# Gated linear attention: the order of full-array and quarter-array products on TensorE

## The chip, the cores and the metric

The kernel runs on one core of a Trainium2 chip. The metric is device time in microseconds (us) of one execution; the median of three runs of the kernel before is 978.45 us. TensorE (PE) multiplies, VectorE (DVE), ScalarE (ACT) and GpSimd (POOL) do the element-wise work, SyncE (SP) issues the DMAs. Each engine has one instruction queue and works it off in order.

## The reference

One layer of a decoder block: a projection, gated linear attention (GLA), block-sparse attention, a merge, cross-attention and a mixture of 32 experts. The change touches GLA alone: 512 rows, 4 heads, keys of 64, values of 128, chunks of 64 rows. Cut to that:

```python
b = jnp.cumsum(log_a, axis=3)
att = jnp.einsum('bhncd,bhnsd->bhncs', q * jnp.exp(b - b_mid), k * jnp.exp(b_mid - b))
att = jnp.where(causal, att, 0.0)
o_intra = jnp.einsum('bhncs,bhnsv->bhncv', att, v)
kv = jnp.einsum('bhncd,bhncv->bhndv', k * jnp.exp(b_last - b), v)
...
_, states = lax.scan(step, init, (jnp.moveaxis(decay, 2, 0), jnp.moveaxis(kv, 2, 0)))
...
o_inter = jnp.einsum('bhncd,bhndv->bhncv', q * jnp.exp(b), states)
o = o_intra + o_inter
```

So a chunk's output is its masked scores times its values, plus its queries times the state that the chunks before it have left. Chunk 0 has no state before it.

## The kernel before

The 512 rows are four tiles (t) of 128, two chunks (c) each. Two heads stand together as a head pair (hp): head 2 hp + half has its 64 key features in partitions 64 half to 64 half + 63. PE's array is 128 by 128: the partitions of the operands are its rows, the partitions of the result its columns. A product whose operands fill 128 partitions and whose result does too takes the full array; the score products take half of the rows (64 partitions in, 128 out); a product with 64 in and 64 out takes a quarter.

`gla()` is a generator. It writes its part of the program in pieces; `weave` puts projection work (`project()`, through `in_feat` and `in_rows`, tiles `fo` and `ro`) between them, as much as the number of each `yield` asks for. The order of the instructions in the queues is the order in which the program is written.

- Scores (lines 547 to 552): for each half, four products k2 by q1, one for each tile, into a PSUM bank `a_ps` of their own; then `copy_predicated` on DVE puts the masked scores into `att[hp]`.
- States (lines 563 to 575): quarter-array products `kv`, 64 rows (a chunk's half of a tile) by 64 columns (half) for chunks 0 to 6, then a scan on DVE into `st[hp]`.
- Outputs (lines 589 to 616): for each tile t two PSUM banks `o_ps0` and `o_ps1`, one for each half, with both head pairs side by side. For each half and hp there is one full-array product (att by vg, all 128 rows of the tile) and behind it one quarter-array product for each of the tile's two chunks (q3 by st; rows by half, columns by the chunk's place in the tile), which adds to what the full one left. Tile 0 has no product for chunk 0. When a half is done, ACT squares it (line 603); then come the row sums on DVE, the power on POOL (line 608), four scalings into `ot` on DVE (line 611), and, one tile later, `finish`: four transposes `ogt` on PE, split by `og.put` on ACT and DVE.

Weights come through `wload` (DMA into `wraw`, issued by SP), are split into `whi` on ACT and `wlo` on DVE by `wsplit`, and are used two blocks later. `load_bias`, behind `gla`, writes a bias table `tbd` to memory and reads it back as `tbias`. Expert weights (`we`) are issued by `eload` as buffers come free.

Of the kernel before, what the change touches and what calls it, by code (L numbers as in the profile page):

```python
# [21 lines left out]
P = 128  # L22
T = 512
NT = T // P
# [41 lines left out]
def bcast_rows(ap, n):  # L66
    return bass.AP(tensor=ap.tensor, offset=ap.offset, ap=[[0, P], [1, n]])
# [3 lines left out]
def block_kernel(ctx, tc, x, mem, g_mem, rel_bias, g_mix, w_in, w_alpha_up, b_alpha, g_gla_head, w_proj_gla,  # L71
# [4 lines left out]
    V, S, G, PE, SY = nc.vector, nc.scalar, nc.gpsimd, nc.tensor, nc.sync  # L76
# [14 lines left out]
    def blk(name, shape, dt=F32):  # L91
        return bp.tile([P] + list(shape), dt, tag="b", name=name)

    def med(name, shape, dt=F32, parts=P):
        return mp.tile([parts] + list(shape), dt, tag="m", name=name)
# [5 lines left out]
    def ps(name, shape, parts=P):  # L101
        return pp.tile([parts] + list(shape), F32, tag="p", name=name)
# [15 lines left out]
    def rows2(name, n, w=T, dt=F32):  # L118

        per = 1024 // w  # L120
        b = [blk(f"{name}{i}", [per, w], dt) for i in range(-(-n // per))]
        return [b[k // per][:, k % per, :] for k in range(n)]
# [12 lines left out]
    def mm(o, l, r, first=True, last=True, **kw):  # L135
        PE.matmul(o, l, r, start=first, stop=last, **kw)  # L136

    def tcol(t):
        return slice(t * P, (t + 1) * P)
# [129 lines left out]
    gmask = first([4, P], U8)  # L269
# [100 lines left out]
    rg, vg, qk = rows2("rg", NT), rows2("vg", NT), rows2("qk", 4)  # L370
# [120 lines left out]
    def gla():  # L491
        at_ps = ps("at_ps", [T], parts=16)
        for t in range(NT):
            PE.transpose(at_ps[:, tcol(t)], alr[:, t, :], ident)
        alrT = med("alrT", [T], parts=17)
        G.memset(alrT, 1.0)
        V.tensor_copy(alrT[0:16, :], at_ps)
        ghb = med("ghb", [512])
        SY.dma_start(ghb, bcast_rows(g_gla_head, 512))
        yield 2.0  # L500
        loga = blk("loga", [NT, 256])
        zz, ab = [], []
        for i in range(2):
            z_ps = ps("z_ps", [2, 256])
            for j in range(2):
                mm(z_ps[:, j, :], alrT[:, tcol(2 * i + j)], wup)
            zz.append(z_ps.rearrange("p a b -> p (a b)"))
            ab.append(med("tmp", [512]))
            S.activation(ab[i], zz[i], AF.Abs)
        for i in range(2):  # L510
            S.activation(ab[i], ab[i], AF.Exp, scale=-1.0)
        for i in range(2):
            S.activation(ab[i], ab[i], AF.Ln, bias=1.0)
            V.scalar_tensor_tensor(loga[:, 2 * i:2 * i + 2, :].rearrange("p a b -> p (a b)"), zz[i], 0.0, ab[i],
                                   op0=ALU.min, op1=ALU.subtract)
        att = [blk(f"att{i}", [2, NT, P]) for i in range(2)]
        for i in range(2):
            G.memset(att[i], 0.0)
        yield "qk"
        q3, k4s, decs, st = [None] * 2, [None] * 2, [None] * 2, [None] * 2  # L520

        def c3(ap):
            return ap.rearrange("p (c t) -> p c t", t=64)

        for hp in range(2):
            b_ps = ps("b_ps", [T])
            for t in range(NT):
                mm(b_ps[:, tcol(t)], loga[:, t, tcol(hp)], tri)
            b_sb, dm, q1, k2 = rows2(f"gw{hp}", 4)
            q3[hp] = med("q3", [512])  # L530
            k4s[hp] = k4 = med("k4", [512])
            S.activation(b_sb, b_ps, AF.Copy, scale=1.0 / 16.0)
            bv = c3(b_sb)
            V.tensor_tensor(c3(dm), bv, bv[:, :, 31:32].to_broadcast([P, 8, 64]), op=ALU.subtract)
            S.activation(q1, dm, AF.Exp)
            S.activation(k2, dm, AF.Exp, scale=-1.0)
            V.tensor_tensor(q1, qk[hp], q1, op=ALU.mult)
            V.tensor_tensor(k2, qk[2 + hp], k2, op=ALU.mult)
            V.tensor_tensor(c3(dm), bv[:, :, 63:64].to_broadcast([P, 8, 64]), bv, op=ALU.subtract)
            S.activation(k4, dm, AF.Exp)  # L540
            V.tensor_tensor(k4, qk[2 + hp], k4, op=ALU.mult)
            decs[hp] = dec = small("dec", [8])
            S.activation(dec, bv[:, :, 63], AF.Exp)
            S.activation(q3[hp], b_sb, AF.Exp)
            V.tensor_tensor(q3[hp], qk[hp], q3[hp], op=ALU.mult)
            yield 6.0
            for half in range(2):
                sl = slice(64 * half, 64 * half + 64)
                a_ps = ps("a_ps", [NT, P])
                for t in range(NT):  # L550
                    mm(a_ps[:, t, :], k2[sl, tcol(t)], q1[sl, tcol(t)])
                V.copy_predicated(att[hp][:, half], gmask, a_ps)
            yield 1.0
            kr_ps = ps("kr_ps", [NT, P])
            for t in range(NT):
                PE.transpose(kr_ps[:, t, :], k4[:, tcol(t)], ident)
            kr = med("kr", [NT, P])
            V.tensor_copy(kr, kr_ps)
            yield GF[hp]
            yield "v"  # L560
            st[hp] = blk(f"st{hp}", [8, P])
            kv_ps = [ps(f"kv{i}", [4, P]) for i in range(2)]
            for c in range(7):
                rs = slice(64 * (c % 2), 64 * (c % 2) + 64)
                for half in range(2):
                    h = 2 * hp + half
                    mm(kv_ps[c % 2][64 * half:64 * half + 64, c // 2, :], kr[rs, c // 2, 64 * half:64 * half + 64],
                       vg[c // 2][rs, tcol(h)], skip_group_check=True)
            for c in range(7):
                kv = kv_ps[c % 2][:, c // 2, :]  # L570
                if c == 0:
                    V.tensor_copy(st[hp][:, 1, :], kv)
                else:
                    V.scalar_tensor_tensor(st[hp][:, c + 1, :], st[hp][:, c, :], dec[:, c:c + 1], kv, op0=ALU.mult,
                                           op1=ALU.add)
            yield 2.0
        for t in range(NT):
            G.tensor_tensor(rg[t], rg[t], ghb, op=ALU.mult)

        def finish(t, ot):  # L580
            t_ps = ps("ogt", [4, P])
            for h in range(4):
                PE.transpose(t_ps[:, h, :], ot[:, h, :], ident)
            og.put(0, tcol(t), t_ps)

        og = Feat("og", 4)
        gla_out.append(og)
        prev = None
        for t in range(NT):
            o_ps = [ps(f"o_ps{half}", [2, P]) for half in range(2)]  # L590
            sq = med("tmp", [4, P])
            for half in range(2):
                sl = slice(64 * half, 64 * half + 64)
                for hp in range(2):
                    h = 2 * hp + half
                    o = o_ps[half][:, hp, :]
                    mm(o, att[hp][:, half, t, :], vg[t][:, tcol(h)], True, False, skip_group_check=True)
                    for c in (2 * t, 2 * t + 1):
                        if c:
                            rs = slice(64 * (c % 2), 64 * (c % 2) + 64)  # L600
                            mm(o[rs], q3[hp][sl, c * 64:(c + 1) * 64], st[hp][sl, c, :], False, c == 2 * t + 1,
                               skip_group_check=True)
                S.activation(sq[:, half:4:2, :], o_ps[half], AF.Square)
            ss = small("ss4", [4])
            V.tensor_reduce(ss, sq, axis=AX.X, op=ALU.add)
            V.tensor_scalar(ss, ss, 1.0 / 128, EPS, op0=ALU.mult, op1=ALU.add)
            rr = small("rr4", [4])
            G.tensor_tensor(rr, ss, neghalf, op=ALU.pow)
            ot = med("ot", [4, P])
            for h in range(4):  # L610
                V.scalar_tensor_tensor(ot[:, h, :], o_ps[h % 2][:, h // 2, :], rr[:, h:h + 1], rg[t][:, tcol(h)],
                                       op0=ALU.mult, op1=ALU.mult)
            yield 2.5
            if prev:
                finish(*prev)
            prev = (t, ot)
        yield 2.0
        finish(*prev)

    fill = project()  # L620
    weave(gla(), fill)
    load_bias()
    drain(fill)
# [103 lines left out]
    for ii in range(4):  # L727
# [4 lines left out]
        for a in range(2):  # L732
            i = 2 * ii + a
# [3 lines left out]
            o = ps("fo", [T])  # L737
            drain(feat(o, gh[:, :, tcol(a)], gl_[:, :, tcol(a)], og.hi, og.lo))
            V.tensor_tensor(zg[i], o, zg[i], op=ALU.mult)
            o = ps("fo", [T])  # L740
# [712 lines left out]
```

## Time and profile before

| | us |
|---|---|
| median of 3 runs (978.40 to 978.49) | 978.45 |
| the profiled execution | 977.96 |
| its span, first to last instruction | 976.1 |
| PE busy | 956.1 (98%) |
| DVE busy | 471.6 (48%) |
| ACT busy | 312.4 (32%) |
| granted TensorE clock, mean | 0.996 |

The span is 1.86 us shorter than the time of the same execution. In a row of the timeline the first number is the start in us from the span's beginning, the second the time from there to the end of the group's last instruction; matmuls are pipelined, so the next row on PE can start before that end, and the difference of two starts is what a group costs. xN counts instructions: a float32 product is two passes on PE, and each is an instruction. In a row of the windows view stand the stretch, its length, then each engine's busy time with the number of instructions, then the granted clock, the busy share of the DMA engines and GB/s. The granted clock is 1.00, the upper of TensorE's two levels, in all stretches used here.

### The profile page before, as it was taken

Reading aid. Unit: us, or ns where it says so; the run is one execution under the profiler, and the core shown is the slowest. Engines: PE = TensorE matmul, PEld = TensorE weight load, DVE = VectorE, ACT = ScalarE, POOL = GpSimd, SP = SyncE. Lnnn points to the kernel's source line nnn. Section 1 sums busy time; section 2 is a strip of 40 time slices with the busy share of each in tenths; the row PEclk is TensorE's granted clock in tenths of the full one; section 3 lists DMA queues with packets and bytes.
Section 4 is the critical chain, followed back from the end, with each engine's and each line's share of the span. In section 5 each row is a group of like instructions: output and inputs, shape, how many; then the busy total and the mean of one; then the engine's idle time right before and its main releaser. Section 6 shows DMA issues by size and latency. Waiting matters only on the chain.

```text
span 976.1 us, 13247 instructions
## 1 busy us (share of the span) xinstructions
PE 956.1 (98%) x4969; PEld 622.3 (64%) x4969; DVE 471.6 (48%) x1047; ACT 312.4 (32%) x639; POOL 32.6 (3%) x46
## 2 busy tenths in 40 slices
PE   8999999999999999999989999999999999999995
PEld 7888778878888888888834445454454543545432
DVE  5344863455556845566743255342544414345224
ACT  6452633445555434465421101111021111201103
POOL 3200010000000000000000000000000000000003
PEclk9999999999999999999999999999999999999998
DMA  9512347223153504473689999999999999999983
GB/s 299 165 44 65 65 58 188 58 80 93 59 181 126 194 25 126 141 264 146 248 313 409 409 409 409 409 409 409 409 409 409 409 409 408 409 409 409 409 319 135
DMA packets 114086, 252.47 MB, mean 259 GB/s; under 512 B 10310, under 2 KB 55651, under 8 KB 114020
## 3 DMA queue, kind: packets, MB, share of 16 engines
q1 hardware_dynamic: 113444, 250.55, 69.8%
q10 hardware_dynamic: 576, 1.05, 0.3%
q8 instruction: 40, 0.66, 0.3%
q14 instruction: 26, 0.21, 0.1%
HBM read 247.90 MB, written 3.67 MB: 258 GB/s over the span
## 4 chain that ended last, share of the span: by engine, by line
PE 92%; DVE 3%; ACT 3%; issue 1%; DMA 1%; SPq 0%; ACTq 0%; POOL 0%; DVEq 0%
PE gu_ps L136 22%; PE y_ps L136 12%; PE fo L131 7%; PE fo L132 7%; PE fo L133 7%; PE g_ps L136 7%; PE c_ps L136 6%; PE ro L133 2%; PE ro L131 2%; PE ro L132 2%; PE x2o L136 2%; PE xo L132 1%; PE xo L133 1%; PE xo L131 1%; PE o_ps L136 1%; PE mo_ps L136 1%
## 5 line engine op out<-in xcount | busy, mean ns | idle before, releaser
L136 PE MATMUL gu_ps<-we,xT 128*64 128x512 f32 x1024 | 229.2, 595 | 1.3 <-DMA we<-in_w_exp_up_dram 0.7
L136 PEld LDWEIGHTS gu_ps<-we,xT 128*64 128x64 f32 x1024 | 70.9, 137 | 135.3 <-issue 121.8
L206 DVE TENSOR_TENSOR wlo<-wraw,whi 128x1024 fp32r<-128x1024 f32 (+1 forms) x71 | 86.0, 1231 | 74.5 <-ACT whi L205 74.3
L136 PE MATMUL y_ps<-we,hid_t 128*64 128x512 f32 x512 | 114.2, 596 | 0.7 <-ACT hid_t L1235 0.7
L1227 DVE SCALAR_TENSOR_TENSOR hid<-hid,ws,gu_ps 128x512 f32<-128x512 f32 x16 | 12.0, 747 | 172.3 <-PE gu_ps L136 172.3
L131 PE MATMUL fo<-hTh,whi 128*128 128x512 f32 x224 | 89.1, 398 | 0.0
L133 PE MATMUL fo<-hTh,wlo 128*128 128x512 f32 x224 | 87.5, 390 | 0.0
L132 PE MATMUL fo<-hTl,whi 128*128 128x512 f32 x224 | 87.5, 390 | 0.0
L1260 DVE TENSOR_TENSOR x<-c_ps,x 128x512 f32<-128x512 f32 x120 | 75.0, 682 | 20.7 <-PE c_ps L136 20.7
L136 PEld LDWEIGHTS y_ps<-we,hid_t 128*64 128x64 f32 x512 | 35.8, 137 | 69.8 <-issue 61.1
L205 ACT ACTIVATE whi<-wraw 128x1024 fp32r<-128x1024 f32 (+2 forms) x73 | 74.4, 1044 | 1.0 <-DMA wraw<-in_w_in_dram 0.7
L136 PE MATMUL g_ps<-oh,xrh 128*128 128x256 f32 x256 | 66.0, 299 | 1.4 <-DVE oh L1025 1.4
L136 PEld LDWEIGHTS g_ps<-oh,xrh 128*128 128x128 f32 x256 | 47.0, 189 | 30.7 <-issue 24.3
L136 PE MATMUL g_ps<-oh,xrl 128*128 128x256 f32 x256 | 61.6, 281 | 0.0
L1226 ACT ACTIVATE hid<-gu_ps 128x512 f32<-128x512 f32 x16 | 9.6, 597 | 157.9 <-PE gu_ps L136 157.9
L205 ACT ACTIVATE yh<-y_ps 128x512 fp32r<-128x512 f32 x32 | 19.1, 598 | 115.1 <-PE y_ps L136 115.1
L1200 ACT ACTIVATE xT<-g_ps,gfeat 128x256 f32<-128x256 f32 x56 | 25.8, 474 | 89.2 <-PE g_ps L136 57.6
L136 PE MATMUL c_ps<-yh,ot 128*128 128x512 f32 x128 | 51.9, 406 | 0.7 <-ACT yh L205 0.7
L136 PE MATMUL c_ps<-yl,ot 128*128 128x512 f32 x128 | 50.6, 395 | 0.2 <-DVE yl L206 0.2
L131 PEld LDWEIGHTS fo<-hTh,whi 128*128 128x128 f32 x224 | 42.1, 188 | 10.1 <-issue 1.9
L133 PEld LDWEIGHTS fo<-hTh,wlo 128*128 128x128 f32 x224 | 42.0, 188 | 9.1
L136 PEld LDWEIGHTS g_ps<-oh,xrl 128*128 128x128 f32 x256 | 47.1, 189 | 0.6
(321 smaller groups left out, 1499.6 us busy)
## 6 DMA issues: line engine op xcount, KB each, us to landing
we<-in_w_exp_gate_dram SPq DMA_DIRECT2D x128, 512.0 KB, 10.2
we<-in_w_exp_up_dram SPq DMA_DIRECT2D x128, 512.0 KB, 10.2
we<-in_w_exp_down_dram SPq DMA_DIRECT2D x128, 512.0 KB, 10.2
wraw<-in_w_in_dram SPq DMA_DIRECT2D x38, 512.0 KB, 3.8
wraw<-in_w_out_dram SPq DMA_DIRECT2D x8, 512.0 KB, 5.0
wraw<-in_w_ckv_dram SPq DMA_DIRECT2D x8, 512.0 KB, 5.1
wraw<-in_w_proj_gla_dram SPq DMA_DIRECT2D x4, 512.0 KB, 4.2
wraw<-in_w_proj_moba_dram SPq DMA_DIRECT2D x4, 512.0 KB, 4.2
```

The source lines that it names most:

```text
L131: PE.matmul(o, lh, rh, start=first, stop=False)
L132: PE.matmul(o, lh, rl, start=False, stop=False)
L133: PE.matmul(o, ll, rh, start=False, stop=last)
L136: PE.matmul(o, l, r, start=first, stop=last, **kw)
L205: S.activation(hi, src, AF.Copy)
L206: eng.tensor_tensor(lo, src, f(hi), op=ALU.subtract)
L1200: S.activation(xT[k], o, AF.Copy, scale=gfeat[:, k:k + 1])
L1226: S.activation(row, gu[0][0:n], AF.Silu)
L1227: V.scalar_tensor_tensor(row, row, ws[:, 0:1], gu[1][0:n], op0=ALU.mult, op1=ALU.mult)
L1260: V.tensor_tensor(xs, o, xs, op=ALU.add)
```

## The change

In the scores both halves' banks are taken first, and the halves alternate from product to product; the mask copies follow when all eight products are written. In the outputs a tile's four full-array products come first, and all its quarter-array products after them. These are ordered by hp, then i, then half, with the chunk chosen so that the two of a step differ in rows (half) and in columns (chunk's place). The squares follow at the end of the tile, one half after the other. The accumulation flags change with it: the first full product of a bank starts it, and the others add. No instruction is added or taken away, and DVE, ACT, POOL and SP keep theirs in the same order.

```diff
@@ -544,12 +544,13 @@
-            for half in range(2):
-                sl = slice(64 * half, 64 * half + 64)
-                a_ps = ps("a_ps", [NT, P])
-                for t in range(NT):
-                    mm(a_ps[:, t, :], k2[sl, tcol(t)], q1[sl, tcol(t)])
-                V.copy_predicated(att[hp][:, half], gmask, a_ps)
+            a_ps = [ps("a_ps", [NT, P]) for half in range(2)]
+            for t in range(NT):
+                for half in range(2):
+                    sl = slice(64 * half, 64 * half + 64)
+                    mm(a_ps[half][:, t, :], k2[sl, tcol(t)], q1[sl, tcol(t)])
+            for half in range(2):
+                V.copy_predicated(att[hp][:, half], gmask, a_ps[half])
@@ -589,17 +590,19 @@
             sq = med("tmp", [4, P])
+            for hp in range(2):
+                for half in range(2):
+                    mm(o_ps[half][:, hp, :], att[hp][:, half, t, :], vg[t][:, tcol(2 * hp + half)], hp == 0, False,
+                       skip_group_check=True)
+            for hp in range(2):
+                for i in range(2):
+                    for half in range(2):
+                        c = 2 * t + (i + half) % 2
+                        sl, rs = (slice(64 * a, 64 * a + 64) for a in (half, c % 2))
+                        if c:
+                            mm(o_ps[half][rs, hp, :], q3[hp][sl, c * 64:(c + 1) * 64], st[hp][sl, c, :], False, True,
+                               skip_group_check=True)
             for half in range(2):
-                sl = slice(64 * half, 64 * half + 64)
-                for hp in range(2):
-                    h = 2 * hp + half
-                    o = o_ps[half][:, hp, :]
-                    mm(o, att[hp][:, half, t, :], vg[t][:, tcol(h)], True, False, skip_group_check=True)
-                    for c in (2 * t, 2 * t + 1):
-                        if c:
-                            rs = slice(64 * (c % 2), 64 * (c % 2) + 64)
-                            mm(o[rs], q3[hp][sl, c * 64:(c + 1) * 64], st[hp][sl, c, :], False, c == 2 * t + 1,
-                               skip_group_check=True)
                 S.activation(sq[:, half:4:2, :], o_ps[half], AF.Square)
```

PE's queue at the score products of head pair 0, before (-) and now (+); the number behind a_ps names the bank, one for each half (a row is a product):

```order
 L133 MATMUL ro1_691<-whi_660,hTl1_150 128x512
-L136 MATMUL a_ps_761<-gw01_709 128x128 x4
-L136 MATMUL a_ps_767<-gw01_709 128x128 x4
+L136 MATMUL a_ps_761<-gw01_709 128x128
+L136 MATMUL a_ps_762<-gw01_709 128x128
+L136 MATMUL a_ps_761<-gw01_709 128x128
+L136 MATMUL a_ps_762<-gw01_709 128x128
+L136 MATMUL a_ps_761<-gw01_709 128x128
+L136 MATMUL a_ps_762<-gw01_709 128x128
+L136 MATMUL a_ps_761<-gw01_709 128x128
+L136 MATMUL a_ps_762<-gw01_709 128x128
```

Four products of one half and then four of the other have become eight that alternate; head pair 1 has the same.

PE's queue at output tile 1, before (128x128 is a full-array product, 64x128 a quarter-array one):

```order
L136 MATMUL o_ps0_1168<-vg0_155,att0_577 128x128
L136 MATMUL o_ps0_1168<-st0_869,q3_710 64x128 x2
L136 MATMUL o_ps0_1168<-vg0_155,att1_578 128x128
L136 MATMUL o_ps0_1168<-st1_1072,q3_912 64x128 x2
L136 MATMUL o_ps1_1169<-vg0_155,att0_577 128x128
L136 MATMUL o_ps1_1169<-st0_869,q3_710 64x128 x2
L136 MATMUL o_ps1_1169<-vg0_155,att1_578 128x128
L136 MATMUL o_ps1_1169<-st1_1072,q3_912 64x128 x2
```

And PE's queue at the same tile now:

```order
L136 MATMUL o_ps0_1168<-vg0_155,att0_577 128x128
L136 MATMUL o_ps1_1169<-vg0_155,att0_577 128x128
L136 MATMUL o_ps0_1168<-vg0_155,att1_578 128x128
L136 MATMUL o_ps1_1169<-vg0_155,att1_578 128x128
L136 MATMUL o_ps0_1168<-st0_869,q3_710 64x128
L136 MATMUL o_ps1_1169<-st0_869,q3_710 64x128
L136 MATMUL o_ps0_1168<-st0_869,q3_710 64x128
L136 MATMUL o_ps1_1169<-st0_869,q3_710 64x128
L136 MATMUL o_ps0_1168<-st1_1072,q3_912 64x128
L136 MATMUL o_ps1_1169<-st1_1072,q3_912 64x128
L136 MATMUL o_ps0_1168<-st1_1072,q3_912 64x128
L136 MATMUL o_ps1_1169<-st1_1072,q3_912 64x128
```

Four changes between a full product and quarter ones and back have become one; tiles 2 and 3 have the same, and tile 0 half of the quarter products.

## Rows read from the trace of the kernel before

**Rows 1.** The page's chain that ended last, shares by engine:

```profile
PE 92%; DVE 3%; ACT 3%; issue 1%; DMA 1%; SPq 0%; ACTq 0%; POOL 0%; DVEq 0%
```

**Rows 2.** Windows: length; busy (instructions) of PE, weight loads, DVE, ACT, POOL; clock, DMA:

```profile
117.00:142.00 25.00, 25.00 (x148) 18.05 (x147) 16.66 (x39) 10.49 (x21) 4.05 (x4) 1.00 0.45 51
...
490.00:495.00 5.00, 4.65 (x34) 3.31 (x36) 3.54 (x15) 3.46 (x9) 0.00 (x0) 1.00 0.22 66
...
500.00:900.00 400.00, 398.38 (x1998) 185.50 (x1996) 162.32 (x337) 57.52 (x108) 0.00 (x0) 1.00 1.03 408
```

**Rows 3.** Timeline of PE, scores of head pair 0: start, time, what:

```profile
72.10 1.71 PE L136 MATMUL a_ps<-gw 64*128 64x128 f32 x16
73.74 0.50 PE L131 MATMUL ro<-whi,hTh 128*128 128x512 f32 x1
```

**Rows 4.** Windows of a_ps on PE alone; (x) counts the passes in flight:

```profile
72.60:72.64 0.04, 0.04 (x2) 1.00 0.00 0
72.90:72.94 0.04, 0.04 (x5) 1.00 0.00 0
```

**Rows 5.** Timeline of PE, output tiles 0 and 1:

```profile
117.59 0.38 PE L136 MATMUL o_ps<-vg,att 128*128 128x128 f32 x2
117.90 0.43 PE L136 MATMUL o_ps<-st,q 64*64 64x128 f32 x2
118.26 0.49 PE L136 MATMUL o_ps<-vg,att 128*128 128x128 f32 x2
...
120.59 0.50 PE L131 MATMUL fo<-hTh,whi 128*128 128x512 f32 x1
...
123.47 0.38 PE L136 MATMUL o_ps<-vg,att 128*128 128x128 f32 x2
123.78 0.43 PE L136 MATMUL o_ps<-st,q 64*64 64x128 f32 x4
124.14 0.49 PE L136 MATMUL o_ps<-vg,att 128*128 128x128 f32 x2
124.56 0.44 PE L136 MATMUL o_ps<-st,q 64*64 64x128 f32 x4
...
126.50 0.50 PE L131 MATMUL fo<-hTh,whi 128*128 128x512 f32 x1
```

**Rows 6.** Timeline of PE: full-array products b_ps, quarter-array products kv, what follows them:

```profile
64.30 1.05 PE L136 MATMUL b_ps<-first,loga 128*128 128x128 f32 x8
65.11 0.48 PE L131 MATMUL ro<-whi,hTh 128*128 128x512 f32 x1
...
89.40 1.09 PE L136 MATMUL kv<-vg,kr 64*64 64x128 f32 x28
90.42 0.50 PE L131 MATMUL fo<-hTh,whi 128*128 128x512 f32 x1
```

**Rows 7.** Timelines of DVE and PE: scalings and transposes of tiles 0 and 3:

```profile
124.83 1.13 DVE L611 SCALAR_TENSOR_TENSOR ot<-o_ps,rr,rg 128x128 f32<-128x128 f32 x4 [1.13 <-POOL rr L608]
129.38 0.60 PE L583 MATMUL ogt<-keep,ot 128*128 128x128 f32 x4
...
139.17 0.50 PE L131 MATMUL fo<-hTh,whi 128*128 128x512 f32 x1
141.72 1.13 DVE L611 SCALAR_TENSOR_TENSOR ot<-o_ps,rr,rg 128x128 f32<-128x128 f32 x4 [1.12 <-POOL rr L608]
145.24 0.60 PE L583 MATMUL ogt<-keep,ot 128*128 128x128 f32 x4
```

**Rows 8.** Waits of SP (us, times, longest); timelines of DVE and PE behind them:

```profile
SPq L442 <- DMA tbd<-tb: 32.9, 1, 32.9
...
155.41 4.63 DVE L206 TENSOR_TENSOR wlo<-wraw,whi 128x1024 fp32r<-128x1024 f32 x4
168.83 0.39 PE L131 MATMUL ro<-whi,hTh 128*128 128x512 f32 x1
```

**Rows 9.** The chain that ended last, in order of time, at its end:

```profile
937.33 8.06 DMA we<-in_w_exp_up_dram
```

## The prediction

> **What bounds the kernel now.** I read the chain of waits first: TensorE (PE) holds 92% of the work that ended last [rows 1]. The busy times by stage then say where that matters for this change: from 117 to 142 us, the stage of the output tiles, PE is busy for all of its 25 us [rows 2]. So PE time that is taken out of this stage comes off the path as long as the engines and the transfers that feed PE keep up; how they stand is looked at below. PE's timeline then gives the two places that the change touches: the score products, 1.64 us for each head pair (72.10 to 73.74) [rows 3], and the output tiles, 3.00 us for tile 0 (117.59 to 120.59) and 3.03 us for tile 1 (123.47 to 126.50) [rows 5]; tiles 2 and 3 show the pattern of tile 1. Together that is 2 x 1.64 + 3.00 + 3 x 3.03 = 15.4 us, the most that the change can act on. A float32 product is two passes on PE in the trace: the 8 score products stand there as x16.
>
> **Output tiles: what a switch costs.** In tile 1, two passes of a full-array product take 0.31 us up to the start of the quarter-array ones (123.47 to 123.78), the four quarter passes behind them take 0.36, and the next full product, which comes straight after quarter ones, takes 0.42 (124.14 to 124.56) [rows 5]. Eight full passes with nothing between them take 0.81 us from their start to the next block's (64.30 to 65.11) [rows 6], 0.10 to 0.11 each. So of the 0.42 only 0.22 is two passes at that pace; the rest is emptying the array and loading weights that could not be loaded ahead. A tile pays that at all of its four full and four quarter groups; after the change it has one group of each.
>
> **Output tiles: what is left.** Full part: 0.31 for the first two passes with the switch at the end, and six more at 0.11: 0.97 us. Quarter part: I need the time of n passes in one quarter while the other three work too. With n = 2 it is 0.36, and it is 0.36 both in tile 0, where one quarter works (117.90 to 118.26), and in tile 1, where two do [rows 5]. The state products kv are the nearest row for all four quarters at once: 14 products, 28 passes, in 1.02 us (89.40 to 90.42) [rows 6]. The even chunks, of which there are four, give 8 passes to each of two quarters, so n = 8 takes 1.02. The slope is (1.02 - 0.36) / 6 = 0.11 us a pass, and n = 4 takes 0.58. A changed tile 1, 2 or 3 has 8 quarter products over four quarters, so n = 4; tile 0 has four products over two quarters, n = 4 too. A tile is then 0.97 + 0.58 = 1.55 us. Saved: 1.45 in tile 0 and 3 x 1.48 in the others, **5.9 us**. The bounds: kv as it stands is the best case; the worst that a row bears out is that only two quarters go on together, as the pairs of before do, and then tiles 1 to 3 have eight passes in line, 1.02 instead of 0.58, which takes 1.3 us back. I take the kv value, because kv has the same shape (64 rows, 64 columns, 128 wide), the same two banks by row half, and neighbours that change quarter at each product.
>
> **Scores.** Before, one row half's eight passes come ahead of the other's. PE overlaps them in part already: at 72.60 us two passes are in flight, at 72.90 five [rows 4]. One half alone, straight after full-array work, would take 0.42 for two passes and 6 x 0.11 for the rest, 1.08 us; the measured 1.64 is that plus 0.56 in which the second half had not begun. With alternating halves both begin together: 1.08 us, 0.56 saved for each pair, **1.1 us** in all. Bounds: nothing, if the five in flight are already all that PE takes, and 1.1; five passes in flight from two halves is what two full streams look like (two to three each), so I take 1.1. The mask copies on VectorE (DVE) wait for the end of each half; that end moves for the second half by 0.56 to the front and for the first hardly.
>
> **What the new order makes later.** The square of half 0 on ScalarE (ACT) could start before half 1 was multiplied; now both wait for the end of the tile, so the second runs behind the first, 0.4 us. Behind them on ACT stand the evacuations of the projection, and behind the row sums on DVE, the power on GpSimd and the four scalings on DVE stands the transpose (ogt) on PE. In tile 3 that chain ran from the end of the products (139.17) to 142.85 (141.72 + 1.13), 3.7 us, and PE asked for it at 145.24 [rows 7]: 2.4 us of cover, 2.0 after the change, if DVE is free. It is not wholly free: tile 0's scalings end at 125.96 (124.83 + 1.13) behind a weight split on DVE that does not move, and PE, which asked at 129.38, will ask 2.9 us earlier, at 126.45 [rows 7]. That is 0.5 us of cover. By the same count (each DVE step of this stretch laid end to end) the last tile's scalings come out about when PE asks. I take off 0.1 us, with 0 and 0.5 as ends. If the cover were gone by more, PE's in-order queue would hold the projection's matmuls behind ogt.
>
> **Does the gain last to the end.** Two things do not move with PE. First, the write of the bias table: SyncE's queue (SP) waits 32.9 us for it, with the next weight loads behind it; DVE had split a batch of four blocks, the first of those loads among them, by 160.04 (155.41 + 4.63), and PE begins on the first of those loads at 168.83 [rows 8]. With PE 6.9 us ahead that is 161.9, still 1.9 us after the whole batch is ready. Second, the expert weights: from 500 to 900 us the DMA moves 408 GB/s with a share of 1.03, while PE is busy 398.38 of 400 [rows 2]; both are full. What counts is what starts that stream. From 490 to 495 us it carried only 66 GB/s [rows 2], so it had run dry and was waiting for buffers; an earlier PE starts it earlier. The last loads (8.06 us from 937.33) stand on the chain [rows 9] behind the branch that PE has to reach first, so they move as well. Everything behind 160 us should shift as a block.
>
> **Sum.** 5.9 + 1.1 - 0.1 = 6.9 us. The profiled execution took 977.96 us, of which 976.1 is the span; it becomes 971.1 with a span of 969.2. The median of the runs is 0.49 above the profiled one, so the forecast is 978.45 - 6.9, about **971.5 us**.
>
> **Rivals.**
> *Two quarters at a time.* The four quarters pair up only by row half or only by column, tiles 1 to 3 take 0.97 + 1.02 = 1.99 us, and the gain is 5.6: 972.9. For it: before shows no more than pairs in these tiles. Against it: kv. The Trainium skill ("TensorE: Matmul & The Clock Gate", Part 3, The mechanism) says that weight loads overlap running matmuls only when their row groups differ, so that two quarters of one row half would go one after the other. The trace does not agree: four passes in two quarters of one row half took the 0.36 that two passes in one took [rows 5].
> *Given back downstream.* The expert stream or the bias table holds the end where it is, and PE waits instead: about 978.3, no change. For it: 1.03 of DMA share for 400 us [rows 2]. Against it: the dry spell at 490 us, and 1.9 us of cover at the bias table. A part given back would lie at 973.5 to 976.
> *Every neighbour empties the array.* If a product that shares neither rows nor columns with the one before had to wait for it, a quarter product would cost its lone 0.36 and a score product 0.42: tile 1 takes 0.97 + 8 x 0.36 = 3.85, tile 0 2.41, the scores 8 x 0.42 = 3.36 each. That is 3 x 0.82 - 0.59 + 2 x 1.72 = 5.3 us more, 983.8: slower. It decides against the change from (3.03 - 0.97) / 8 = 0.26 us a quarter product on. Against it: kv has such neighbours (the last quarter of one chunk and the first of the next) and takes 1.02 / 14 = 0.07 a product.
> *The scores gain nothing*, because PE already overlaps what it can: 972.6, inside the range.
>
> **How the numbers follow.** Forecast 0.79 (with the scores' bound in it), two at a time 0.08, a part given back 0.03, all given back 0.07, slower 0.03. A measurement of this kernel tells about 0.2%, 2 us, from no change. Faster is then 0.79 + 0.08 + 0.03 = 0.90, the same 0.07, slower 0.03. The range goes from 970.9 (0.6 below the forecast: each slope 0.02 smaller, no wait at ogt, the spread of runs) to 973.6 (two at a time, with the larger wait at ogt).
>
> **What would show it.** Right: a score group of about 1.08 us, each output tile at about 1.55 us up to the next projection matmul, PE with no more than 0.2 us of idle time from 117 to 142, 490 to 495 us of before found again some 7 us earlier, and all later stages as long as they were. Wrong: quarter passes that need about 1.0 us a tile (two at a time); PE waiting at ogt for the scalings; PE waiting for weights behind 150 us or in the expert stage, with the last load landing where it did.

## The result, and the profile after

The changed kernel takes 970.34 us (median; 969.94 to 971.04) against 978.42 us for the kernel before (978.17 to 978.49) on the same chip: a ratio of 0.9923, with a 95% interval of 0.9911 to 0.9936. It is faster by 8.1 us, where 6.9 were forecast; the median lies 0.56 us under the range, whose lower end was 970.9. The interval, 6.3 to 8.7 us, holds both 6.9 and 8.1. The profiled execution took 969.94 us with a span of 968.1, 8.0 us less than the one of before.

What the change touches came out as forecast. PE's timeline of the changed kernel at the first score group and at output tiles 0 and 1 (start, time to the end of the group, what):

```profile
72.09 1.16 PE L136 MATMUL a_ps<-gw 64*128 64x128 f32 x16
73.19 0.50 PE L131 MATMUL ro<-whi,hTh 128*128 128x512 f32 x1
...
116.48 1.05 PE L136 MATMUL o_ps<-vg,att 128*128 128x128 f32 x8
117.47 0.65 PE L136 MATMUL o_ps<-st,q 64*64 64x128 f32 x8
118.05 0.50 PE L131 MATMUL fo<-hTh,whi 128*128 128x512 f32 x1
...
120.91 1.05 PE L136 MATMUL o_ps<-vg,att 128*128 128x128 f32 x8
121.89 0.67 PE L136 MATMUL o_ps<-st,q 64*64 64x128 f32 x16
122.49 0.50 PE L131 MATMUL fo<-hTh,whi 128*128 128x512 f32 x1
```

From the start of a group to the start of the next: a score group takes 1.10 us against 1.64 [rows 3], tile 0 1.57 against 3.00 and tile 1 1.58 against 3.03 [rows 5]. The first projection matmul behind tile 3 stood at 139.17 [rows 7] and now stands at 132.26:

```profile
132.26 0.50 PE L131 MATMUL fo<-hTh,whi 128*128 128x512 f32 x1
```

PE is 6.91 us ahead there, and it stays so: the dry stretch of the expert stream and the 400 us behind it, found 6.92 us earlier, show the busy times, clock and GB/s of before [rows 2] (windows of the changed kernel; columns as in [rows 2]):

```profile
483.08:488.08 5.00, 4.65 (x34) 3.31 (x36) 3.54 (x15) 3.46 (x9) 0.00 (x0) 1.00 0.24 65
493.08:893.08 400.00, 398.38 (x1998) 185.50 (x1996) 162.38 (x337) 57.51 (x108) 0.00 (x0) 1.00 1.03 409
```

The rest appears only behind 925 us, in the last group of gate and up products (gu_ps), where PE waits for the last expert weights. PE's timeline of the kernel before, a part of it that was not shown above; in brackets the idle time of PE ahead of a group and what ended it:

```profile
932.07 11.32 PE L136 MATMUL gu_ps<-we,xT 128*64 128x512 f32 x50
943.67 1.08 PE L136 MATMUL gu_ps<-we,xT 128*64 128x512 f32 x4 [0.28 <-DMA we<-in_w_exp_gate_dram]
945.43 2.79 PE L136 MATMUL gu_ps<-we,xT 128*64 128x512 f32 x10 [0.68 <-DMA we<-in_w_exp_up_dram]
948.15 0.50 PE L136 MATMUL c_ps<-yh,ot 128*128 128x512 f32 x1
```

The same stretch of the changed kernel:

```profile
925.15 15.02 PE L136 MATMUL gu_ps<-we,xT 128*64 128x512 f32 x64
940.10 0.50 PE L136 MATMUL c_ps<-yh,ot 128*128 128x512 f32 x1
```

The group took 948.15 - 932.07 = 16.08 us and now takes 14.95. That is 1.13 us, and 6.92 + 1.13 = 8.05, the whole difference between the two profiled executions. The granted clock is 1.00 throughout the group in both, so it is not the clock. The question for the experiments is whether this 1.1 us belongs to the change.

### The profile page after: what moved, and what is told of

It reads as the page before. It is cut to its first block, busy times and chain, and to the rows that moved or that the text cites. A ratio compares the mean times of both kernels' runs of the same rounds, so it can differ in the third digit from the quotient of the medians.

```text
span 968.1 us, 13248 instructions
## 1 busy us (share of the span) xinstructions
PE 949.3 (98%) x4969; PEld 619.2 (64%) x4969; DVE 471.4 (49%) x1047; ACT 312.2 (32%) x639; POOL 32.6 (3%) x46
## 4 chain that ended last, share of the span: by engine, by line
PE 92%; DVE 3%; ACT 3%; DMA 1%; issue 1%; ACTq 0%; SPq 0%; DVEq 0%
PE gu_ps L136 22%; PE y_ps L136 12%; PE fo L131 8%; PE fo L133 7%; PE fo L132 7%; PE g_ps L136 7%; PE c_ps L136 6%; PE ro L133 3%; PE ro L131 3%; PE ro L132 3%; PE x2o L136 2%; PE xo L132 1%; PE xo L133 1%; PE xo L131 1%; PE mo_ps L136 1%; PE s_ps L136 1%
```

## The experiments

**Theory A**: the change gives 6.9 us of PE time; what lies beyond is chance of the single execution, above all in the wait for the last weights. The rivals put the surplus into the output tiles, the scores, or into something that does not move with PE. The medians below are those of all executions of a kernel beside the kernel before on the same chip.

| kernel | median (lowest to highest), us | ratio to before, 95% |
|---|---|---|
| before, beside the next four | 977.62 (976.45 to 979.42) | |
| outputs alone | 972.65 (971.34 to 973.30) | 0.9935 to 0.9962 |
| after, delayed | 977.01 (976.40 to 978.51) | 0.9987 to 1.0005 |
| before, early branch | 977.33 (977.08 to 979.14) | 0.9990 to 1.0008 |
| after, early branch | 970.92 (970.05 to 971.25) | 0.9917 to 0.9945 |
| before, beside the next four, another chip | 977.75 (976.57 to 978.97) | |
| after again | 971.06 (970.91 to 971.79) | 0.9919 to 0.9946 |
| scores alone | 976.88 (975.78 to 978.93) | 0.9984 to 1.0002 |
| before, early loads | 975.21 (975.17 to 975.79) | 0.9965 to 0.9985 |
| after, early loads | 968.37 (968.30 to 968.66) | 0.9890 to 0.9920 |

The first thing to see is the kernel before itself: on both chips its executions spread over more than 2 us, not over the 0.1 us of the three runs that the prediction started from.

### The two parts alone

Outputs alone is the change without the part on the scores:

```diff
-            a_ps = [ps("a_ps", [NT, P]) for half in range(2)]
-            for t in range(NT):
-                for half in range(2):
-                    ...
+            for half in range(2):
+                ...
+                for t in range(NT):
+                    mm(a_ps[:, t, :], k2[sl, tcol(t)], q1[sl, tcol(t)])
```

> Only the output tiles are in the new order; the scores are as before. The changed kernel's trace shows tiles of 1.57 and 1.58 us (116.48 to 118.05, 120.91 to 122.49) and PE 6.91 us ahead of before from 139 us on up to 943 us; the rest of its 8.1 us comes in the wait for the last loads of expert weights behind the branch (PE waits 0.28 and 0.68 us there before, nothing after). Theory A (the surplus is that wait, it depends on when the loads meet PE, and it differs from one execution to the next): PE is 5.82 us ahead at 142 us, and the time is 971.0 with no wait at the end and up to 972.7 with the longest wait, 1.7 us. Rival B (the surplus sits in the output tiles or in something that they shift): 978.4 - 5.8 - 1.1 = 971.5 or less in every execution. Rival C (it comes with the scores): 972.6. The tiles themselves should stand at 1.57 to 1.58 us by each.

Scores alone is the reverse, the kernel before with only the part on the scores.

> Only the scores are in the new order. In the changed kernel each score group takes 1.10 us (72.09 to 73.19) against 1.64 before. Theory A: PE is 1.09 us ahead behind 103 us, the time 1.1 us under that of the kernel before on the same chip, give or take 0.5 for the chance at the end. Rival (the scores bring the surplus): 2.2 us or more under before. Rival (the scores gain nothing without the outputs): no change, groups of 1.10 us all the same but given back before 117 us.

Each part keeps its own time without the other. PE's timeline of scores alone, at the first group:

```profile
72.13 1.16 PE L136 MATMUL a_ps<-gw 64*128 64x128 f32 x16
73.22 0.50 PE L131 MATMUL ro<-whi,hTh 128*128 128x512 f32 x1
```

and of outputs alone, the start of tile 1 and what follows it:

```profile
122.52 1.05 PE L136 MATMUL o_ps<-vg,att 128*128 128x128 f32 x8
...
124.09 0.50 PE L131 MATMUL fo<-hTh,whi 128*128 128x512 f32 x1
```

That is 1.09 us for the score group and 1.57 for the tile. The medians, 5.0 and 0.9 us under before, go with 5.8 and 1.1 but can't prove them: the interval of scores alone includes no change. Outputs alone speaks against a surplus of 1.1 us in the tiles (rival B asked for 971.5 or less in every execution, and four of five were above); scores alone, against one in the scores (its rival asked for 2.2 us or more under before, and the interval ends at 1.6). In the profiled execution of scores alone the last gu_ps group took 945.97 - 930.98 = 14.99 us, with the outputs in the order of before: so a short group occurs without the new order of the outputs.

The profiled execution of outputs alone also showed a second place where executions differ. A window of outputs alone near the start (columns as in [rows 2]; the granted clock is the third number from the end):

```profile
14.00:16.00 2.00, 2.00 (x11) 2.00 (x10) 2.00 (x2) 1.44 (x2) 0.00 (x0) 0.50 0.94 327
```

PE had waited 0.59 and 0.65 us for split weights, and its clock then stood at 0.50, the lower of the two levels (1.2 GHz), from 14 to 16 us. In the profiled execution of before it had waited 0.68 and 0.50 us, and the clock was 1.00 there; what decides between the two stays open. The same matmul stood at 19.35 in the kernel before and at 19.95 here (PE's timelines, before first):

```profile
19.35 0.39 PE L133 MATMUL ro<-whi,hTl 128*128 128x272 f32 x1 [0.21 <-DVE hTl L326]
```

```profile
19.95 0.28 PE L133 MATMUL ro<-whi,hTl 128*128 128x272 f32 x1
```

So 0.6 us come and go ahead of 20 us, in code that the change does not touch. Behind tile 3 PE was therefore 5.30 us ahead here (133.87 against 139.17), not the 5.82 expected.

### The old place in time, with the new order

```diff
             sq = med("tmp", [4, P])
+            for i in range(31 if t == 0 else 0):
+                mm(o_ps[i % 2][:, 0, :], att[0][:, 0, i % 4, :], vg[0][:, tcol(i % 4)], skip_group_check=True)
             for hp in range(2):
```

> The changed kernel with 31 more full-array products (62 passes of 0.111 us, 6.9 us) ahead of output tile 0, into banks that the tile's first products start anew, so that everything behind 120 us stands where it stood in the kernel before. Theory A (the wait at the end is chance from one execution to the next, or depends on how the loads meet PE): 976.8 with no wait, up to 978.5 with 1.7 us, executions spread over more than 0.5 us. Rival D (the wait hangs on the absolute time, on something that does not move with PE): the wait of before comes back, 1.1 to 1.7 us in every execution, 978.0 to 978.5. Rival B (the new order itself has removed it): no wait, 976.8 to 977.3, as after less the delay.

The executions lie between 976.40 and 978.51, spread over 2.1 us, with a median of 977.01. Rival D (the wait of before in every execution, 978.0 or more) falls, since 8 of the 11 lie under 977.5; on this chip the kernel before does not have it in every execution either, with a median of 977.62. Rival B is not borne out: three lie above its 977.3 by 0.4 us and more. But the interval against before, from 1.3 us under to 0.5 over, can't tell a surplus of 1.1 us from none. In the profiled one the last gu_ps group took 946.90 - 932.27 = 14.63 us:

```profile
932.27 14.70 PE L136 MATMUL gu_ps<-we,xT 128*64 128x512 f32 x64
946.90 0.50 PE L136 MATMUL c_ps<-yh,ot 128*128 128x512 f32 x1
```

### Taking the wait away: an earlier branch, which failed

SyncE (SP) issues the last loads of gate and up weights behind a branch (for experts with too many tokens) that it reaches long before PE does. `SPILL` names the pair of experts, the step of the branch in it, and how many loads go out ahead of it. In both kernels that branch was put one step earlier:

```diff
-SPILL = 15, 2, 372
+SPILL = 15, 1, 372
```

> The kernel before with the branch for overflowing experts one step (8 matmuls, 1.73 us) earlier in the last pair, so that SyncE issues the last loads some 1.7 us earlier. Theory A (the surplus is the wait for these loads): PE's waits of 0.28 and 0.68 us near 943 us are gone or nearly, and the time falls by 1.1 to 1.7 us, to 976.8 to 977.3, with less spread. Rival (the surplus is somewhere else, or the loads are held by the transfers ahead of them and not by the issue): 978.4, no change.

> The changed kernel with the branch one step (1.73 us) earlier. Theory A: the executions above 969.9 come down to it (median 0.4 us lower, 969.9, spread under 0.4), and the distance to the kernel before with the same edit is 6.9 us, PE's own gain. Rival (the surplus of 1.1 us is somewhere else): 970.3 and 8.1 us from the kernel before with the same edit.

Neither came true: 977.33 and 970.92, where 976.8 to 977.3 and 969.9 were expected. They are 6.41 us apart, nearer to theory A's 6.9 than to 8.1. PE's timeline of the kernel before with that edit, in the slowest of its eleven executions:

```profile
932.13 1.89 PE L136 MATMUL gu_ps<-we,xT 128*64 128x512 f32 x8
935.29 9.63 PE L136 MATMUL gu_ps<-we,xT 128*64 128x512 f32 x42 [1.27 <-PEq L1264]
945.35 1.08 PE L136 MATMUL gu_ps<-we,xT 128*64 128x512 f32 x4 [0.43 <-DMA we<-in_w_exp_gate_dram]
946.62 2.79 PE L136 MATMUL gu_ps<-we,xT 128*64 128x512 f32 x10 [0.20 <-DMA we<-in_w_exp_up_dram]
949.34 0.50 PE L136 MATMUL c_ps<-yh,ot 128*128 128x512 f32 x1
```

The idle time for weights shrank (0.63 in sum instead of 0.96), but PE now stood for 1.27 us at the branch itself, where its own sequencer (PEq) released it; in the kernel before no such wait shows there. The group took 949.34 - 932.13 = 17.21 us in this execution, longer than the 16.08 of before. A new wait had come in, so this pair did not decide.

### Taking the wait away: earlier loads

Here the branch stays, and the four loads go out ahead of it:

```diff
-SPILL = 15, 2, 372
+SPILL = 15, 2, 376
```

> The changed kernel with the four last loads of gate and up weights (372 to 375) issued ahead of the branch instead of behind it; SyncE is blocked at the branch for 6.8 us before, so they can go out some 4 to 8 us earlier. Theory A (the wait for these loads is the chance part at the end): no wait of PE for expert weights near 936 us, the last gu_ps group 13.7 to 15.0 us long with no gap, 969.9 us, with a spread of the start alone, under 0.8 us. Rival (the wait comes from the transfers and not from the late issue): gaps of 0.3 to 1.7 us stay, 970.3 or more.

> The same edit in the kernel before: four last loads of gate and up weights ahead of the branch. Theory A: 976.8 to 977.0 us (977.96 less the waits of 0.28 and 0.68 us and the clock's ripple behind them), and 6.9 us from the changed kernel with the same edit, since the chance at the end is gone in both. Rival (the change itself gives 8.1 us): 8.1 us between the two.

This decides, for the chip that it ran on (where the two kernels without the edit are 6.69 us apart, as shown further down). The spread is down to 0.4 and 0.6 us, and the medians are 975.21 - 968.37 = **6.84 us** apart, PE's own gain. The rival's 8.1 falls. PE's timelines of the two, after first:

```profile
925.21 13.90 PE L136 MATMUL gu_ps<-we,xT 128*64 128x512 f32 x64
939.04 0.50 PE L136 MATMUL c_ps<-yh,ot 128*128 128x512 f32 x1
```

```profile
932.55 13.90 PE L136 MATMUL gu_ps<-we,xT 128*64 128x512 f32 x64
946.38 0.50 PE L136 MATMUL c_ps<-yh,ot 128*128 128x512 f32 x1
```

The group takes 13.83 us in both. Measured against that, the profiled executions with late loads lost 16.08 - 13.83 = 2.25 us (before), 1.12 (after) and 0.80 (after, delayed). The idle time in brackets (0.96 in before) had shown less than half of it, since a PE with a pass in flight counts as busy while the next pass waits for its weights. SP's timeline shows the edit: with early loads the last of them goes out at 923.81, against 929.93 in the changed kernel (early loads first):

```profile
923.81 0.33 SPq L938 DMA_DIRECT2D we<-in_w_exp_up_dram  x1
```

```profile
929.93 0.38 SPq L938 DMA_DIRECT2D we<-in_w_exp_up_dram  x1
```

The loads of the down weights behind them are issued earlier too (from 928.39 instead of 930.40). The first 24 passes of the last down products (y_ps), to the next group's start, take 948.68 - 943.38 = 5.30 us with early loads and 950.31 - 944.43 = 5.88 without.

So both kernels get faster, by more than was expected (969.9 and 976.8 to 977.0): I had counted only the idle time in brackets. With early loads the changed kernel, at 968.37 us, is the fastest of all, 9.4 us under the kernel before on the same chip.

### The changed kernel again

> The changed kernel once more, to measure its distance to the kernel before over many executions on one chip; the kernel before has spread over 976.45 to 979.42 us in 21 executions beside the runs of the first experiments. Theory A (the change gives 6.9 us of TensorE time and nothing else; what lies beyond is chance of the single execution, in the wait for the last expert weights and in the first 20 us): the medians lie 6.9 us apart, give or take 0.5. Rival (the change gives 8.1 us): 8.1, give or take 0.5. In the trace PE stands 6.9 us ahead from 140 to 940 us by both, unless the start differs.

971.06 against 977.75: 6.69 us, where theory A said 6.9 and the rival 8.1. The ratio's interval, 0.9919 to 0.9946, is 5.3 to 7.9 us. In this execution the wait was there, with the new order, at its place in the program (PE's timeline; the group takes 941.48 - 925.59 = 15.89 us):

```profile
925.59 11.32 PE L136 MATMUL gu_ps<-we,xT 128*64 128x512 f32 x50
937.49 1.08 PE L136 MATMUL gu_ps<-we,xT 128*64 128x512 f32 x4 [0.58 <-DMA we<-in_w_exp_gate_dram]
...
941.48 0.50 PE L136 MATMUL c_ps<-yh,ot 128*128 128x512 f32 x1
```

The chain that ended last has the last load of up weights in this execution too (issue, time to landing):

```profile
930.60 8.12 DMA we<-in_w_exp_up_dram
```

So the group takes 14.95 and 15.89 us in two executions of one program: a surplus of this size comes and goes without any edit. That load accounts for it. It landed 13.32 us behind the start of the group in before (937.33 + 8.06 - 932.07 [rows 9]), 12.19 in after (929.93 + 7.41 - 925.15) and 13.13 here, and the group lost 2.25, 1.12 and 2.06 us against 13.83: each time 11.07 less. The profiled executions of outputs alone and scores alone give 11.06 and 11.07. What makes the load land sooner or later in one execution than in another stays open. So does how much of the 8.1 us belongs to the chip of the result, where four executions of before lay within 0.3 us of each other: the record does not name that chip, and no later run is known to be from it.

### Which part of the new order gives the gain

Three kernels keep the full products first and reorder the quarter ones. Rows shared has the order of before, half by half:

```diff
-            for hp in range(2):
-                for i in range(2):
-                    for half in range(2):
-                        c = 2 * t + (i + half) % 2
+            for half in range(2):
+                for hp in range(2):
+                    for i in range(2):
+                        c = 2 * t + i
```

> The changed kernel with its quarter products in the order of before (half, then hp, then chunk), behind the full ones: neighbours share the rows, and the four products of half 0 come ahead of those of half 1. The changed order takes 0.60 us for the quarter part of tiles 1 to 3 (121.89 to 122.49). Theory A (a quarter starts when its own work comes up in the queue, and PE takes only so many passes at once, as in the scores of before, where half 1 began 0.56 late): half 1 begins late, the part takes 0.8 to 1.0 us, the tile 1.8 to 2.0. Rival (the order of the quarter products is of no matter, the gain is all from putting the full ones first): 0.60 us, tile 1.58. Rival (the four quarters go on two at a time unless neighbours differ in both): 1.02 us, tile 2.0.

Columns shared runs over i, hp, half, and same quarter over half, i, hp, with c = 2 t + i in both.

> The changed kernel with neighbours that differ in rows and share the columns: chunk, then hp, then half. Theory A (limited number of passes in flight): as with shared rows, 0.8 to 1.0 us for the quarter part, since the second pair of quarters comes only behind four products. Rival (only shared rows disturb): 0.60 us. Rival (order of no matter): 0.60 us here and with shared rows too.

> The changed kernel with the two products of each quarter (four passes) next to each other: half, chunk, hp. Theory A (limited number of passes in flight, each quarter one after the other in itself): the worst order of the four, between the pairs' 0.8 and the sum of four quarters' own four passes, 4 x 0.49 = 1.96 us. Rival (order of no matter): 0.60 us.

PE's timelines of rows shared, columns shared and same quarter, the quarter part of tile 1 and what follows it:

```profile
122.53 0.68 PE L136 MATMUL o_ps<-st,q 64*64 64x128 f32 x16
123.14 0.50 PE L131 MATMUL fo<-hTh,whi 128*128 128x512 f32 x1
```

```profile
121.88 0.68 PE L136 MATMUL o_ps<-st,q 64*64 64x128 f32 x16
122.49 0.50 PE L131 MATMUL fo<-hTh,whi 128*128 128x512 f32 x1
```

```profile
122.64 0.69 PE L136 MATMUL o_ps<-st,q 64*64 64x128 f32 x16
123.26 0.50 PE L131 MATMUL fo<-hTh,whi 128*128 128x512 f32 x1
```

The quarter parts take 0.61, 0.61 and 0.62 us, against 0.60 in the changed kernel. Theory A's numbers here (0.8 to 1.96) were wrong. The order of the quarter products, half of what the change is about, is worth 0.01 to 0.02 us a tile. These three kernels and the next were executed once each, in 971.42 to 972.45 us against 979.02 for before on their chip; these times can't separate orders that differ by so little, the timelines do.

The last kernel keeps the quarter order and undoes the full-first one by half: two full products, their quarter ones, and the same again, for each head pair.

> The changed kernel with each tile in two groups, one for each head pair: two full products, their four quarter products, and the same again, so one change from quarter to full work more in each tile. By the terms of the sum: two full products 0.53 us at the start (two passes with the switch 0.31, two at 0.11), quarter part of two passes in each of four quarters 0.36, full products after quarter ones 0.64 (0.42 and 0.22), quarter part 0.36: 1.89 us a tile against 1.58, and PE 0.3 us a tile behind the changed kernel, 0.9 to 1.2 in all. Rival (the number of changes is of no matter, the quarter order alone gives the gain): 1.58 us.

```profile
121.32 0.61 PE L136 MATMUL o_ps<-vg,att 128*128 128x128 f32 x4
121.86 0.45 PE L136 MATMUL o_ps<-st,q 64*64 64x128 f32 x8
122.24 0.71 PE L136 MATMUL o_ps<-vg,att 128*128 128x128 f32 x4
122.88 0.45 PE L136 MATMUL o_ps<-st,q 64*64 64x128 f32 x8
123.26 0.50 PE L131 MATMUL fo<-hTh,whi 128*128 128x512 f32 x1
```

0.54 + 0.38 + 0.64 + 0.38 = 1.94 us a tile, where 1.89 was worked out. So the gain of the tiles follows the number of groups, counted in pairs of one full and one quarter group: from four pairs to two it is 3.03 - 1.94 = 1.09 us, 0.55 for each, and from two to one 0.36. In the first step a quarter group also goes from two quarters at work (0.36 us) to four (0.38); the two were not taken apart.

A rival that no experiment was made for is a wait of each quarter product for the full product that it adds to. The rows speak against it. In before the first quarter pass adds to the full product right ahead of it and starts 0.31 - 0.11 = 0.20 us behind that product's last pass [rows 5]; in the changed kernel it adds to a product that is four back and starts 0.98 - 7 x 0.11 = 0.21 behind the last full pass.

## Why the prediction was off, step by step

- **PE bounds the program, and its time comes off the path**: right. PE was 6.91 us ahead at 132.26, and the two kernels with early loads are 6.84 us apart.
- **Output tiles, 5.9 us**: 3.00 + 3.03 + 3.04 + 3.03 = 12.10 became 1.57 + 1.58 + 1.59 + 1.58 = 6.32, so 5.78. The terms of a tile were 0.97 and 0.58; they measured 0.98 and 0.60. The kv products were the right row for four quarters at once.
- **Scores, 1.1 us**: 2 x 0.54 = 1.08. The step from "five in flight" to "two full streams" held.
- **Stall at ogt, 0.1 us**: there is none, and the working was wrong twice. PE came at 125.35, 4.03 us earlier than before and not 2.9: I had left out the 1.1 us of the scores. With scalings that end at 125.96, as I had it, PE would have stood for 0.6 us. But the split of weights that I thought fixed moved too: it starts at 120.81 instead of 121.67 and ends at 122.04, and tile 0's scalings behind it end at 123.97 + 1.12 = 125.09 instead of 125.96. The two errors offset each other, which is luck. Timeline of DVE, then of PE, in the changed kernel:

```profile
120.81 1.23 DVE L206 TENSOR_TENSOR wlo<-wraw,whi 128x1024 fp32r<-128x1024 f32 x1
...
123.97 1.12 DVE L614 SCALAR_TENSOR_TENSOR ot<-o_ps,rr,rg 128x128 f32<-128x128 f32 x4 [1.13 <-POOL rr L611]
```

```profile
125.35 0.60 PE L584 MATMUL ogt<-keep,ot 128*128 128x128 f32 x4
```

- **The bias table does not give the gain back**: right, PE is still 6.92 us ahead at 925.15. **Everything behind 160 us shifts as a block**: right up to 925 us, and this is where the prediction failed. I argued from the one chain of before that the last loads stand behind the branch "so they move as well" [rows 9], and took their 8.06 us as a constant. It is 7.41 in the changed kernel's chain:

```profile
929.93 7.41 DMA we<-in_w_exp_up_dram
```

and it was issued 4.78 us behind the start of the group instead of 5.26. Issue and landing give 0.48 + 0.65 = 1.13 us, the whole surplus of the profiled pair. What PE lost in that group went from 0.80 us (after, delayed) to 2.25 (before) in the profiled executions above.
- **The range**: the 0.6 us below the forecast were to hold, among other things, "the spread of runs". It came from three runs of before that agreed within 0.1 us; 21 later runs spread over 3 us. [rows 9] showed that a transfer stood on the chain, though not how much PE lost to it; with a loss that turned out to lie between 0.80 and 2.25 us, the range needed 1 us or more on either side whatever the slopes were. Its upper end does not come out of its terms either: two at a time with 0.5 us at ogt is a gain of 5.9 - 1.3 + 1.1 - 0.5 = 5.2 us and gives 973.25, not 973.6. The forecast of the difference was right, 6.9 against 6.84 with early loads in both kernels; the 8.1 of the result held 1.2 us beyond that, 1.13 of it, in the profiled pair, in the wait for the last load.
- **The rivals**: two quarters at a time (1.99 us a tile) falls with 1.58, and with neighbours that share rows the quarter part takes 0.61 us instead of 0.60. The rule of the Trainium skill ("TensorE: Matmul & The Clock Gate", Part 3, The mechanism) that weight loads overlap running matmuls only when their row groups differ doesn't agree with the 0.61. Given back downstream falls with 6.84. Every neighbour empties the array falls with 1.58.

## What to carry to other kernels

Count the changes between products of different shapes on the array, and put those of one shape together: each pair of groups (one full, one quarter) that was saved gave 0.36 to 0.55 us a tile here, while the order among the small ones was worth 0.02. Where the chain of waits ends in a transfer that one execution shows, treat its length as a range, and look whether it can be issued ahead of the branch or wait that holds it: that gave 2.5 to 2.7 us here, with one number changed. To measure a gain of this size, first take away the wait that scatters the runs, in both kernels.

## What the runs showed of the hardware

- Four quarters of the array worked side by side in all four orders tried: 16 passes took 0.60 to 0.62 us, in the last order with four passes of one quarter in a row. In the scores of before eight passes of one half stood in a row, and the second half began only between 72.60 and 72.68, 0.50 to 0.58 us behind the first: two passes started within 0.04 us there, while one half starts one each 0.11 us (windows of a_ps on PE, columns as in [rows 4]; at 72.60 there were two). At that pace the first half can't start its eighth pass before 72.10 + 7 x 0.11 = 72.87, so passes of the second half start ahead of passes that stand before them in the queue; the statement at the beginning that an engine works its queue off in order does not hold for PE to that point. How many passes in a row hold up the other parts was not tried between these two cases, four of a quarter and eight of a half.

```profile
72.64:72.68 0.04, 0.04 (x4) 1.00 0.00 0
```

- PE's idle time understates a wait for data while passes are in flight: 0.96 us in brackets where the group took 2.25 us longer than with early loads.
- A branch one step earlier cost PE 1.27 us at the branch itself. Why it does so there, and not at the old place, stays open.
